# Gates and the retention half of the output projection by seven block products instead of eight

## The chip, the cores and the metric

The kernel runs on one core of one Trainium2 chip. The metric is the device time of one execution in microseconds (us). Of three runs of the kernel before the median is 1057.25 us (1056.99 to 1058.26).

## The reference, cut to what matters

One encoder layer on 1024 tokens of width 1024, all float32:

```python
h = rms_norm(x, norm_w) * (1 + scale) + shift          # adaLN(c) gives shift, scale, gate
r_q, r_k, r_v, r_g, m_cq, m_ckv, m_kr, m_g = split_cols(h @ w_in, SPLIT_SIZES)
# group A: 8 retention heads, both directions, group norm, then
ret_out = o * silu(r_g)                                # r_g: 1024 columns
# group B: latent attention with 8 heads
cq, ckv = rms_norm(m_cq, q_norm_w), rms_norm(m_ckv, kv_norm_w)     # 384 and 256 columns
q, kv = cq @ w_uq, ckv @ w_ukv                         # then per-head norms, rotary, softmax
mla_out = rms_norm(att, mla_out_norm_w) * silu(m_g)    # m_g: 1024 columns
x = x + gate * (concatenate([ret_out, mla_out]) @ w_out)
```

## The kernel before, in words

Every float32 product is made of three TensorE products of rounded halves: `split` (lines 75 to 82) makes a high part on ScalarE (line 80) and the rest, the low part, on GpSimd or VectorE (line 81); `mm3` (lines 64 to 67) then adds high x high, high x low and low x high into one accumulator. The accumulators are the eight banks of PSUM: four under the tag `acc`, four under `sm`. `h` lies in SBUF, feature by token, as eight pairs `hh`, `hl` of 128 x 1024. Weight pages come through `wpage` (line 84): load into `wr` (two buffers), split into `wh` and `wl` (seven buffers each), all in the pool `ring`.

The stages in order: the features `h` and the first retention projection (to about 82 us); four retention groups of two heads (line 330), each with a loop over eight token tiles (line 336: projection of 24 products, rotary, scores, states), a reverse scan over the states (line 397), the retention gate (from line 404: two pages, 96 products of 128 x 512, SiLU into `sg`), and the output part (line 416: two halves of four tiles; statistics, normalisation, transposes, line 444 multiplies by the gate, and the result goes to DRAM as `retD`). Then the latents (line 505: `cq` with 384 columns, `ckv` with 288, per token tile 24 products, norm, four transposes, high and low part into `cqh`, `cql`, `ckh`, `ckl`, which stay in SBUF). The eight latent gates (`mla_gate`, line 449) are written down in two parts, before and after the latents; they go to DRAM as `mgD`. `gate_column` (line 496) multiplies eight 512 KB pages on VectorE for the adaLN gate. Then the retention half of the output projection (line 557: `retD` is loaded and split, 8 x 2 x 24 products, residual added, stored as `xyD`), the pages of `w_uq` and `w_ukv` (line 577), the up-projections (line 595; lines 606 and 616 take the tag `wr` for the squares), attention, and the second half of the output projection.

The order written down is not the order issued: at the end a planner simulates the program, and each engine's stream is arranged by what is ready in that simulation, earlier lines first. Engines then work their streams strictly in order. SP issues the loads and most stores, ScalarE some stores. Pools are stacks from the left and the right end of SBUF; a pool that is opened where a closed one lay waits, tile by tile, for the tiles whose bytes it takes (`reuse_waits="tile"`).

## Time and profile before

| | |
|---|---|
| median of three runs | 1057.25 us |
| profiled execution | 1057.49 us |
| its span, first to last instruction | 1055.3 us |
| TensorE products (PE) | 1018.1 us busy, 5736 products |
| VectorE (DVE) | 581.4 us busy |
| ScalarE (ACT) | 426.0 us busy |
| GpSimd (POOL) | 404.1 us busy |
| mean granted clock of TensorE | 0.988 |

A product's row gives its latency; the next one starts before it ends, so rates are read from starts. PEld is the weight load, which overlaps the products. Behind a group's or an instruction's time stands the idle time of its engine before it, and what ended it.

### The profile page before, as it was taken

How to read it: one execution, taken by the hardware profiler on the slowest of the kernel's cores; microseconds unless marked ns; L12 is line 12 of the kernel's file. 1: busy time of each engine (PE TensorE's matmuls, PEld its weight loads, DVE VectorE, ACT ScalarE, POOL GpSimd, SP SyncE). 2: the span in 40 equal slices, each digit the busy share in tenths (PEclk: the TensorE clock that was granted, in tenths of full speed). 3: DMA queues.
4: the chain of work that ended last, by engine and by line, in shares of the span. 5: the costliest groups of instructions: out<-in, count | busy, mean ns of one | idle time of the engine just before them, and what ended most of it. 6: DMA issues, size and time to landing. Idle time of an engine off the chain costs nothing.

```text
span 1055.3 us, 15223 instructions
## 1 busy us (share of the span) xinstructions
PE 1018.1 (96%) x5736; PEld 888.3 (84%) x5736; DVE 581.4 (55%) x1390; ACT 426.0 (40%) x800; POOL 404.1 (38%) x311
## 2 busy tenths in 40 slices
PE   5899999999999999999999999989999999989998
PEld 4687887888888888998888889879889999878887
DVE  7996546444643534336302116777877777883342
ACT  6654213312321322124322006577767776772100
POOL 2233315213411411224633217943466555873210
PEclk8899999999999999999999999999999999998999
DMA  9721103101110212224654520100000000003522
GB/s 365 264 64 57 41 1 120 41 2 62 63 36 20 85 47 73 102 84 136 201 171 153 183 85 11 41 1 2 20 21 21 2 20 22 21 20 120 169 101 70
DMA packets 30744, 82.27 MB, mean 78 GB/s; under 512 B 3536, under 2 KB 4560, under 8 KB 30672
## 3 DMA queue, kind: packets, MB, share of 16 engines
q1 hardware_dynamic: 25920, 72.92, 20.4%
q10 hardware_dynamic: 4752, 8.39, 2.2%
q8 instruction: 45, 0.74, 0.3%
q14 instruction: 27, 0.22, 0.1%
HBM read 64.52 MB, written 16.78 MB: 77 GB/s over the span
## 4 chain that ended last, share of the span: by engine, by line
PE 82%; DVE 11%; DMA 2%; ACT 2%; issue 2%; POOL 2%; ACTq 0%; DVEq 0%; POOLq 0%
PE acc L65 13%; PE acc L66 13%; PE acc L67 13%; PE pt L739 4%; PE sp L65 4%; PE sp L66 4%; PE sp L67 4%; PE po L66 3%; PE po L67 3%; PE po L65 3%; DVE x L178 2%; DMA wa<-w_ada 2%; PE sm L425 2%; PE sm L424 1%; PE sm L65 1%
## 5 line engine op out<-in xcount | busy, mean ns | idle before, releaser
L81 POOL TENSOR_TENSOR wl<-wr,wh 128x1024 fp32r<-128x1024 f32 (+2 forms) x51 | 115.2, 2268 | 173.2 <-ACT wh L80 148.9
L65 PE MATMUL acc<-wh,hh 128*128 128x512 f32 (+2 forms) x352 | 130.8, 372 | 1.7 <-ACT hh L189 1.7
L66 PE MATMUL acc<-wl,hh 128*128 128x512 f32 (+2 forms) x352 | 130.3, 370 | 0.0
L67 PE MATMUL acc<-wh,hl 128*128 128x512 f32 (+2 forms) x352 | 126.4, 368 | 2.1 <-DVE hl L190 2.1
L725 POOL TENSOR_SCALAR pr<-pr,st 128x1024 f32<-128x1024 f32 x62 | 72.0, 1165 | 101.1 <-DVE st L724 75.5
L65 PE MATMUL acc<-hh,wh 128*128 128x512 f32 x256 | 101.0, 395 | 1.7 <-ACT v L345 1.7
L742 DVE TENSOR_TENSOR pl<-pt,ph 128x512 fp32r<-128x512 f32 x128 | 85.3, 683 | 31.2 <-ACT ph L741 31.1
L66 PE MATMUL acc<-hl,wh 128*128 128x512 f32 x256 | 100.9, 394 | 0.0
L67 PE MATMUL acc<-hh,wl 128*128 128x512 f32 x256 | 100.6, 393 | 0.0
L80 ACT CAST wh<-wr 128x1024 fp32r<-128x1024 f32 (+2 forms) x55 | 53.8, 982 | 104.1 <-PE sm L66 45.1
L741 ACT CAST ph<-pt 128x512 fp32r<-128x512 f32 x128 | 73.1, 591 | 26.6 <-PE pt L739 24.6
L720 DVE TENSOR_REDUCE st<-sp 128x1 f32<-128x1024 f32 x62 | 75.4, 1216 | 6.5 <-PE sp L67 6.4
L66 PE MATMUL po<-pl,vh 128*128 128x256 f32 x256 | 76.5, 299 | 2.1 <-DVE pl L742 2.0
L723 ACT ACTIVATE pr<-sp,st 128x1024 f32<-128x1024 f32 x62 | 69.5, 1121 | 20.8 <-DVE st L721 20.5
L65 PEld LDWEIGHTS acc<-wh,hh 128*128 128x128 f32 x352 | 67.2, 191 | 10.9 <-ACT hh L189 2.1
L67 PEld LDWEIGHTS acc<-wh,hl 128*128 128x128 f32 x352 | 66.0, 188 | 11.1 <-DVE hl L190 3.0
L66 PEld LDWEIGHTS acc<-wl,hh 128*128 128x128 f32 x352 | 67.3, 191 | 8.7
L739 PE MATMUL pt<-ident,pr 128*128 128x128 f32 x496 | 70.2, 274 | 4.0 <-DVE st L724 2.7
L65 PE MATMUL po<-ph,vh 128*128 128x256 f32 x256 | 73.3, 286 | 0.0
L67 PE MATMUL po<-ph,vl 128*128 128x256 f32 x256 | 72.8, 284 | 0.0
L360 POOL TENSOR_TENSOR rb<-t,t 128x128 f32<-128x128 f32 x32 | 14.8, 464 | 135.0 <-PE sm L370 73.4
L739 PEld LDWEIGHTS pt<-ident,pr 128*128 128x128 f32 x496 | 57.9, 141 | 8.5 <-issue 2.9
(353 smaller groups left out, 2474.2 us busy)
## 6 DMA issues: line engine op xcount, KB each, us to landing
...
retD<-ro SPq DMA_DIRECT2D x16, 256.0 KB, 2.1
...
```

The lines of the kernel that those rows point to most:

```text
L65: T.matmul(out, lh, rh, start=first, stop=False, **kw)
L66: T.matmul(out, lh, rl, start=False, stop=False, **kw)
L67: T.matmul(out, ll, rh, start=False, stop=last, **kw)
L80: A.copy(out=hi, in_=raw)
L81: eng.tensor_tensor(out=lo, in0=raw, in1=hi, op=ALU.subtract)
L178: V.scalar_tensor_tensor(out=wa, in0=wa, scalar=1.0, in1=sc, op0=ALU.mult, op1=ALU.mult, accum_out=mp[:, i:i + 1])
L720: V.tensor_reduce(out=st_[:, 0:1], in_=sp, op=ALU.max, axis=AX.X)
L723: A.activation(pr, sp, AF.Exp, bias=st_[:, 1:2], scale=sc_, accum_out=st_[:, 2:3])
L725: G.tensor_scalar(out=pr, in0=pr, scalar1=st_[:, 3:4], scalar2=0.0, op0=ALU.mult, op1=ALU.add)
L739: T.transpose(tp[:, ts_(q)], pr[:, ts_(half * 4 + q)], ident)
L741: A.copy(out=ph[half][:, :, c_], in_=tv)
L742: V.tensor_tensor(out=pl[half][:, :, c_], in0=tv, in1=ph[half][:, :, c_], op=ALU.subtract)
```

## The change

A product of a 2 x 2 block weight with 2 x 2 blocks of `h` (features 0 to 511 and 512 to 1023, tokens likewise) takes seven block products with sums before and after instead of eight plain ones. This is done for all retention gates, for the latent gates of heads 4 to 7, and for the retention half of the output projection: `block_pair` makes two 128-row output tiles over all tokens, ten times. The block sums on the side of `h`, `U`, are made once, in the latents stage (`combos`, `combo4`), and for the output projection once more from the gated retention (`rgD` in DRAM), written over the same tiles. The latent gates of heads 0 to 3 stay plain products, one page in each retention group. The retention gate is applied in `block_pair`'s stage, to `retD` from DRAM. `gate_column` moves into retention group 2. The latents run half 1 first, are stored to DRAM and loaded again after the output projection; the ring is closed before the latents and opened again after the output projection. The diff, cut to its core:

```diff
-    hh = [p_h.tile([P, S], F32R, name=f"hh{k}", tag=f"hh{k}") for k in range(KT)]
-    hl = [p_h.tile([P, S], F32R, name=f"hl{k}", tag=f"hl{k}") for k in range(KT)]
+
+    hf = [[[p_h.tile([P, 512], F32R, name=f"h{n}{k}{z}", tag=f"h{n}{k}{z}") for n in "hl"] for z in range(2)]
+          for k in range(KT)]
+
+    def h_tok(k, t):
+        return [x[:, ts_(t % 4)] for x in hf[k][t // 4]]
...
+    def gate_column():
+        sc2 = p_ret.tile([P, D], F32, name="sc2", tag="sc2")
+        bcast_row(sc2, sc_col)
+        for k in range(KT):
+            wa = wa_tile(16 + k, p_ret, "wa", 1)
+            V.scalar_tensor_tensor(out=wa, in0=wa, scalar=1.0, in1=sc2, op0=ALU.mult, op1=ALU.mult,
+                                   accum_out=modg[:, k:k + 1])
+        V.tensor_tensor(out=modg, in0=modg, in1=bada[:, 16:24], op=ALU.add)
...
-        wg = [wpage(I["w_rg"][g][j], 1024, 4) for j in range(2)]
-        sg = p_ret.tile([P, 2, S], F32, name="sg", tag="sg")
-        for h in range(2):
-            for half in range(2):
-                ps = acc()
-                for k in range(KT):
-                    wh, wl = wg[k // 4]
-                    rh = hh[k][:, half * 512:half * 512 + 512]
-                    rl = hl[k][:, half * 512:half * 512 + 512]
-                    mm3(ps, wh[:, k % 4, ts_(h)], wl[:, k % 4, ts_(h)], rh, rl, k == 0, k == KT - 1)
-                A.activation(sg[:, h, half * 512:half * 512 + 512], ps, AF.Silu)
+        wg = wpage(I["w_mg1"][g], 1024, KT)
+        for half in range(2):
+            ps = acc()
+            for k in range(KT):
+                mm3(ps, wg[0][:, k], wg[1][:, k], *hf[k][half], k == 0, k == KT - 1)
+            mo = p_ret.tile([P, 512], F32, name="mo", tag="qkT", bufs=2)
+            A.activation(mo, ps, AF.Silu)
+            A.dma_start(out=mgD[g, :, half * 512:half * 512 + 512], in_=mo)
+        if g == 2:
+            gate_column()
...
-                V.scalar_tensor_tensor(out=ro, in0=tp, scalar=gnw[:, 2 * g + h:2 * g + h + 1],
-                                       in1=sg[:, h, half * 512:half * 512 + 512], op0=ALU.mult, op1=ALU.mult)
+                A.activation(ro, tp, AF.Copy, scale=gnw[:, 2 * g + h:2 * g + h + 1])
...
-    for n in range(MG0):
-        mla_gate(n, p_ret, "qkT")
...
+    s_lw = ExitStack()
+    p_r2 = s_lw.enter_context(tc.tile_pool(name="ring2", bufs=1, side="right", reuse_waits="tile"))
+    bn = ("11", "1", "21", "2", "4", "3", "22")
+    p_T = s_h.enter_context(tc.tile_pool(name="pT", bufs=1, side="left", reuse_waits="tile"))
+    U = {"11": [hf[k][0] for k in range(4)], "12": [hf[k][1] for k in range(4)],
+         "21": [hf[k][0] for k in range(4, 8)], "22": [hf[k][1] for k in range(4, 8)]}
+    for n in "123":
+        U[n] = [[p_T.tile([P, 512], F32R, name=f"T{n}{m}{k}", tag=f"T{n}{m}{k}") for m in "hl"] for k in range(4)]
+    U["4"] = U["12"]
+    s_lat = ExitStack()
+    p_lw = s_lat.enter_context(tc.tile_pool(name="latw", bufs=1, side="left", reuse_waits="tile"))
+    cqD = dram.tile([6, P, S], F32R, name="cqD")
+    ckD = dram.tile([4, P, S], F32R, name="ckD")
...
+    def put(dst, x, eng):
+        hi, lo = dst
+        A.copy(out=hi, in_=x)
+        eng.tensor_tensor(out=lo, in0=x, in1=hi, op=ALU.subtract)
+    def tmp(i):
+        return p_lw.tile([P, 512], F32, name=f"x{i}", tag=f"x{i}")
+    def whole(i, blk, k):
+        x = tmp(i)
+        G.tensor_tensor(out=x, in0=U[blk][k][0].bitcast(F32), in1=U[blk][k][1].bitcast(F32), op=ALU.add)
+        return x
+    def combos(k):
+        a, b, d = whole(0, "11", k), whole(1, "12", k), whole(2, "22", k)
+        V.tensor_tensor(out=a, in0=b, in1=a, op=ALU.subtract)
+        put(U["1"][k], a, V)
+        V.tensor_tensor(out=b, in0=d, in1=b, op=ALU.subtract)
+        put(U["3"][k], b, V)
+        V.tensor_tensor(out=d, in0=d, in1=a, op=ALU.subtract)
+        put(U["2"][k], d, V)
+    def combo4(k):
+        a, b = whole(0, "2", k), whole(1, "21", k)
+        V.tensor_tensor(out=a, in0=a, in1=b, op=ALU.subtract)
+        put(U["4"][k], a, V)
+    lat = []
+    for nm, parts_, dd, wts in (("w_cq", ((0, 384),), cqD, qnw), ("w_ckv", ((0, 256), (256, 288)), ckD, kvnw)):
+        w = []
+        for j in range(4):
+            raw = p_r2.tile([P, 2 * n], F32, name="wr", tag="wr", bufs=2)
+            SY.dma_start(out=raw, in_=I[nm][j])
+            w.append(split(raw, (("p (k n) -> p k n",), {"k": 2}), f"{nm}h{j}", f"{nm}l{j}", p_r2))
+        lat.append((n, w, parts_, dd, wts))
+    for half in (1, 0):
...
+                if half == 1 and q % 2 == 1:
+                    combos(2 * unit + q // 2)
+                elif half == 0 and unit == 0:
+                    combo4(q)
...
+                hi = p_lw.tile([P, 512], F32R, name="sth", tag="sth", bufs=2)
+                lo = p_lw.tile([P, 512], F32R, name="stl", tag="stl", bufs=2)
+                A.activation(hi, tp, AF.Copy, scale=wts[:, j:j + 1])
+                V.scalar_tensor_tensor(out=lo, in0=tp, scalar=wts[:, j:j + 1], in1=hi, op0=ALU.mult, op1=ALU.subtract)
+                SY.dma_start(out=dd[j, :, sl].bitcast(F32), in_=hi.bitcast(F32))
+                SY.dma_start(out=dd[nj + j, :, sl].bitcast(F32), in_=lo.bitcast(F32))
+    SY.dma_start(out=tabD[2], in_=krp)
+    s_lat.close()
+    s_lw.close()
...
+    so = ExitStack()
+    p_g = so.enter_context(tc.tile_pool(name="blk", bufs=1, side="right", reuse_waits="tile"))
+    wn = ("11", "S1", "12", "S2", "22", "S3", "S4")
+    W = {}
+    for i, n in enumerate(wn):
+        W[n] = [p_g.tile([P, 4, P], F32R, name=f"W{n}{m}", tag=f"W{n}{m}") for m in "hl"]
+        if i == 1:
+            raws0 = {b: p_g.tile([P, 512], F32, name=f"r{b}", tag=f"r{b}", bufs=2) for b in ("11", "21", "22", "12")}
+    sub, add = ALU.subtract, ALU.add
+    def block_pair(src, consume, raws=None):
+        r = raws or {b: p_g.tile([P, 512], F32, name=f"r{b}", tag=f"r{b}", bufs=2) for b in ("11", "21", "22", "12")}
+        for b in r:
+            SY.dma_start(out=r[b], in_=src[("11", "12", "21", "22").index(b)])
+        def wput(n, x, eng):
+            hi, lo = (y.rearrange("p k n -> p (k n)") for y in W[n])
+            A.copy(out=hi, in_=x)
+            eng.tensor_tensor(out=lo, in0=x, in1=hi, op=sub)
+        s1 = p_g.tile([P, 512], F32, name="ws1", tag="ws1", bufs=1)
+        wput("11", r["11"], G)
+        V.tensor_tensor(out=s1, in0=r["21"], in1=r["22"], op=add)
+        wput("S1", s1, V)
+        V.tensor_tensor(out=r["21"], in0=r["11"], in1=r["21"], op=sub)
+        wput("12", r["12"], G)
+        V.tensor_tensor(out=r["11"], in0=s1, in1=r["11"], op=sub)
+        wput("S2", r["11"], V)
+        wput("22", r["22"], G)
+        wput("S3", r["21"], V)
+        V.tensor_tensor(out=r["12"], in0=r["12"], in1=r["11"], op=sub)
+        wput("S4", r["12"], V)
+        def prod(ps, a, b, first, last):
+            wh, wl = W[a]
+            for k in range(4):
+                mm3(ps, wh[:, k], wl[:, k], *U[b][k], first and k == 0, last and k == 3,
+                    skip_group_check=True)
+        def ot(tag):
+            return p_g.tile([P, 512], F32, name=tag, tag=tag, bufs=1)
+        A_, C_ = acc(), acc()
+        B_, D_ = sm(), sm()
+        prod(A_, "11", "11", True, True)
+        c1 = ot("c1")
+        A.copy(out=c1, in_=A_)
+        prod(C_, "S1", "1", True, True)
+        prod(A_, "12", "21", False, True)
+        consume(0, 0, A_)
+        prod(B_, "S2", "2", True, True)
+        u2, u4 = ot("u2"), ot("u4")
+        V.tensor_tensor(out=u2, in0=c1, in1=B_, op=add)
+        V.tensor_tensor(out=u4, in0=u2, in1=C_, op=add)
+        prod(D_, "22", "4", True, True)
+        prod(B_, "S3", "3", False, True)
+        V.tensor_tensor(out=c1, in0=c1, in1=B_, op=add)
+        c22, c21 = (p_g.tile([P, 512], F32, name="cc", tag="cc", bufs=2) for _ in range(2))
+        V.tensor_tensor(out=c22, in0=c1, in1=C_, op=add)
+        consume(1, 1, c22)
+        V.tensor_tensor(out=c21, in0=c1, in1=D_, op=sub)
+        consume(1, 0, c21)
+        E_ = acc()
+        prod(E_, "S4", "22", True, True)
+        V.tensor_tensor(out=u4, in0=u4, in1=E_, op=add)
+        consume(0, 1, u4)
+    rgD = dram.tile([H, P, S], F32, name="rgD")
...
+    def gate(n0, dst, src):
+        def go(f, z, c_):
+            sl = slice(512 * z, 512 * z + 512)
+            g_ = c_ if c_ is not None and (f or z) else None
+            if g_ is None:
+                g_ = p_g.tile([P, 512], F32, name="cc", tag="cc", bufs=2)
+            A.activation(g_, c_, AF.Silu)
+            if src is not None:
+                ro = io_tile()
+                SY.dma_start(out=ro, in_=src[n0 + f, :, sl])
+                V.tensor_tensor(out=g_, in0=g_, in1=ro, op=ALU.mult)
+            A.dma_start(out=dst[n0 + f, :, sl], in_=g_)
+        return go
+    for i, p_ in enumerate((0, 1, 2, 3)):
+        block_pair(I["w_gb"][p_], gate(2 * p_, rgD, retD), raws0 if i == 0 else None)
+    for p_ in (4, 5):
+        block_pair(I["w_gb"][p_], gate(2 * p_ - 4, mgD, None))
...
+    def ublk():
+        return p_g.tile([P, 512], F32, name="ub", tag="ub", bufs=10)
+    def uload(blk, k):
+        x = ublk()
+        SY.dma_start(out=x, in_=rgD[k + 4 * (blk[0] == "2"), :, slice(0, 512) if blk[1] == "1" else slice(512, 1024)])
+        return x
+    eng = lambda k: V if k % 2 else G
+    t1s = []
+    for k in range(4):
+        a = uload("11", k)
+        put(U["11"][k], a, eng(k))
+        b = uload("12", k)
+        V.tensor_tensor(out=a, in0=b, in1=a, op=sub)
+        t1s.append(a)
+    for k in range(4):
+        put(U["1"][k], t1s[k], eng(k))
+    t2s = []
+    for k in range(4):
+        c = uload("21", k)
+        put(U["21"][k], c, eng(k))
+    for k in range(4):
+        d = uload("22", k)
+        V.tensor_tensor(out=t1s[k], in0=d, in1=t1s[k], op=sub)
+        put(U["2"][k], t1s[k], eng(k))
+    for k in range(4):
+        c = uload("21", k)
+        V.tensor_tensor(out=c, in0=t1s[k], in1=c, op=sub)
+        put(U["4"][k], c, eng(k))
+    for k in range(4):
+        a = uload("11", k)
+        V.tensor_tensor(out=a, in0=t1s[k], in1=a, op=sub)
+        put(U["3"][k], a, eng(k))
+    for k in range(4):
+        put(U["22"][k], uload("22", k), eng(k))
...
+    def residual(f0):
+        def go(f, z, c_):
+            sl = slice(512 * z, 512 * z + 512)
+            xt = io_tile()
+            SY.dma_start(out=xt, in_=I["xT"][f0 + f][:, sl])
+            V.scalar_tensor_tensor(out=xt, in0=c_, scalar=modg[:, f0 + f:f0 + f + 1], in1=xt, op0=ALU.mult, op1=ALU.add)
+            A.dma_start(out=xyD[f0 + f][:, sl], in_=xt)
+        return go
+    for p_ in range(4):
+        block_pair(I["w_ob"][p_], residual(2 * p_))
+    so.close()
     s_h.close()
-    p_o2 = so.enter_context(tc.tile_pool(name="reto2", bufs=1, side="left", reuse_waits="tile"))
-    ohl += [[p_o2.tile([P, S], F32R, name=f"o{n}{k}", tag=f"o{n}{k}") for n in "hl"] for k in range(2, KT)]
-    oh, ol = zip(*ohl)
-    for k in range(KT):
-        raw = raws[k] if k < 2 else p_o.tile([P, S], F32, name="wro", tag="wro", bufs=2)
-        SY.dma_start(out=raw, in_=retD[k])
-        A.copy(out=oh[k], in_=raw)
-        eng = V if k % 2 == 0 else G
-        eng.tensor_tensor(out=ol[k], in0=raw, in1=oh[k], op=ALU.subtract)
-    for f in range(KT):
-        wh, wl = wpage(I["w_out"][f][0], 1024, KT)
-        for z in range(2):
-            sl = slice(z * 512, z * 512 + 512)
-            ps = acc() if z == 0 else sm()
-            for k in range(KT):
-                mm3(ps, wh[:, k], wl[:, k], oh[k][:, sl], ol[k][:, sl], k == 0, k == KT - 1)
-            xt = p_o2.tile([P, 512], F32, name="xt", tag="xt", bufs=4)
-            SY.dma_start(out=xt, in_=I["xT"][f][:, sl])
-            V.scalar_tensor_tensor(out=xt, in0=ps, scalar=modg[:, f:f + 1], in1=xt, op0=ALU.mult, op1=ALU.add)
-            A.dma_start(out=xyD[f][:, sl], in_=xt)
+    s_ck, s_cq = ExitStack(), ExitStack()
+    p_ck = s_ck.enter_context(tc.tile_pool(name="latk", bufs=1, side="right", reuse_waits="tile"))
+    s_ring = ExitStack()
+    p_ring = s_ring.enter_context(tc.tile_pool(name="ring", bufs=7, side="right", reuse_waits="tile"))
+    p_lat = s_cq.enter_context(tc.tile_pool(name="latq", bufs=1, side="right", reuse_waits="tile"))
+    cqh, cql, ckh, ckl = ([pool.tile([P, S], F32R, name=f"{nm}{j}", tag=f"{nm}{j}") for j in range(n)]
+                          for pool, nm, n in ((p_lat, "cqh", 3), (p_lat, "cql", 3), (p_ck, "ckh", 2), (p_ck, "ckl", 2)))
+    for dd, his, los in ((cqD, cqh, cql), (ckD, ckh, ckl)):
+        for j in range(len(his)):
+            SY.dma_start(out=his[j].bitcast(F32), in_=dd[j].bitcast(F32))
+            SY.dma_start(out=los[j].bitcast(F32), in_=dd[len(his) + j].bitcast(F32))
+    krp, mtab["Cq"], mtab["Sq"] = (p_lat.tile([P, NT, 2, 16], F32, name=n, tag=n) for n in ("krp", "Cq", "Sq"))
+    for i, t_ in enumerate((mtab["Cq"], mtab["Sq"], krp)):
+        SY.dma_start(out=t_, in_=tabD[i])
...
+    s_ring.close()
     s_ck.close()
-    s_ring.close()
```

## Rows read from the trace of the kernel before

**Rows 1.** The page's busy times: us (share of the span) xinstructions.

```profile
PE 1018.1 (96%) x5736; PEld 888.3 (84%) x5736; DVE 581.4 (55%) x1390; ACT 426.0 (40%) x800; POOL 404.1 (38%) x311
```

**Rows 2.** The chain of waits on the page, by engine.

```profile
PE 82%; DVE 11%; DMA 2%; ACT 2%; issue 2%; POOL 2%; ACTq 0%; DVEq 0%; POOLq 0%
```

**Rows 3.** Windows: length, busy us (x) of PE, PEld, DVE, ACT, POOL, clock, DMA, GB/s.

```profile
345.00:432.00 87.00, 87.00 (x465) 74.11 (x463) 36.66 (x129) 23.08 (x42) 23.59 (x23) 1.00 0.19 64
432.00:515.00 83.00, 80.88 (x506) 76.94 (x505) 39.23 (x94) 27.43 (x72) 35.46 (x42) 1.00 0.35 117
515.00:635.00 120.00, 120.00 (x534) 99.77 (x533) 17.52 (x20) 22.93 (x28) 34.71 (x16) 1.00 0.47 161
635.00:700.00 65.00, 63.35 (x360) 57.25 (x359) 44.77 (x112) 41.68 (x95) 46.02 (x27) 1.00 0.05 19
```

**Rows 4.** The same window of line 65 alone: products, weight loads.

```profile
345.00:432.00 87.00, 38.19 (x98) 18.24 (x97) 1.00 0.19 64
```

**Rows 5.** Groups of products of the gates and the output: count, busy us, mean ns.

```profile
L65 PE MATMUL acc<-hh,wh 128*128 128x512 f32 x256 | 101.0, 395 | 1.7 <-ACT v L345 1.7
...
L65 PE MATMUL acc<-oh,wh 128*128 128x512 f32 x64 | 24.9, 389 | 0.0
...
L65 PE MATMUL sm<-oh,wh 128*128 128x512 f32 x64 | 24.9, 389 | 0.0
```

**Rows 6.** Timeline of TensorE in the output stage: start, duration.

```profile
545.74 0.39 PE L65 MATMUL acc<-oh,wh 128*128 128x512 f32 x1
...
551.18 0.39 PE L65 MATMUL acc<-oh,wh 128*128 128x512 f32 x1
```

**Rows 7.** Line 565, low parts of 1024 columns: ns min/median/max.

```profile
L565 DVE TENSOR_TENSOR ol<-wro,oh x4: 1224/1225/2107, 519.1 to 562.2; 128x1024 fp32r<-128x1024 f32 x4
...
L565 POOL TENSOR_TENSOR ol<-wro,oh x4: 2387/2400/3371, 521.2 to 565.0; 128x1024 fp32r<-128x1024 f32 x4
```

**Rows 8.** Timeline of VectorE, output part of the last group: start, duration, idle before.

```profile
392.57 0.42 DVE L380 TENSOR_TENSOR sT<-sm,mask 128x256 f32<-128x256 f32 x1 [4.38 <-PE sm L378]
...
401.48 0.49 DVE L430 BATCH_NORM_STATS2 bs<-o 128x6 f32<-128x128 f32 x2 [4.74 <-ACT o L427]
...
413.83 1.41 DVE L444 SCALAR_TENSOR_TENSOR ro<-sm,small,sg 128x512 f32<-128x512 f32 x2 [2.80 <-PE sm L442]
...
419.78 0.49 DVE L430 BATCH_NORM_STATS2 bs<-o 128x6 f32<-128x128 f32 x2 [3.16 <-ACT o L427]
...
430.24 1.41 DVE L444 SCALAR_TENSOR_TENSOR ro<-sm,small,sg 128x512 f32<-128x512 f32 x2 [4.10 <-PE sm L442]
```

**Rows 9.** Timeline of one latent tile, from its squares to its scaled copy.

```profile
446.60 0.49 ACT L524 ACTIVATE jk<-acc 128x384 f32<-128x384 f32 x1 [3.60 <-PE acc L67]
...
448.09 0.62 DVE L531 TENSOR_SCALAR cn<-acc,rr 128x384 f32<-128x384 f32 x1 [0.72 <-POOL rr L528]
```

**Rows 10.** Line 542, high part of a latent on ScalarE: ns min/median/max.

```profile
L542 ACT ACTIVATE ckh<-sm,small x4: 678/680/689, 493.5 to 512.6; 128x512 fp32r<-128x512 f32 x4
```

**Rows 11.** DMA issues: count, KB each, median us from issue to landing.

```profile
retD<-ro SPq DMA_DIRECT2D x16, 256.0 KB, 2.1
...
wr<-w_ukv SPq DMA_DIRECT2D x4, 384.0 KB, 3.1
```

**Rows 12.** Timeline about 505 us: GpSimd and VectorE side by side.

```profile
502.71 4.74 POOL L81 TENSOR_TENSOR wl<-wr,wh 128x1024 fp32r<-128x1024 f32 x2
...
503.45 1.70 DVE L491 TENSOR_TENSOR rp<-cn,Ck 128x32 f32<-128x32 f32 x1
505.07 2.42 DVE L492 TENSOR_TENSOR rp<-cn,Sk 128x32 f32<-128x32 f32 x1
```

**Rows 13.** Line 492, the same multiplication in all token tiles: ns min/median/max.

```profile
L492 DVE TENSOR_TENSOR rp<-cn,Sk x8: 185/186/2423, 485.2 to 509.5; 128x32 f32<-128x32 f32 x8
```

**Rows 14.** Groups by form, splits of 768 columns: count, busy us, mean ns.

```profile
L81 POOL TENSOR_TENSOR wl<-wr,wh 128x768 fp32r<-128x768 f32 x11 | 20.2, 1839 | 77.9 <-ACT wh L80 77.9
...
L80 ACT CAST wh<-wr 128x768 fp32r<-128x768 f32 x11 | 9.2, 837 | 58.9 <-PE sm L66 38.2 <-DMA xt<-xT 10.0 <-DMA wr<-w_uq 6.7
```

88 lines of the change are left out of this document (26 added, 62 removed).

## The prediction, made before the result was known

> **What bounds the kernel now.** I read the busy times first: TensorE is busy 1018.1 of 1055.3 us, VectorE 55%, ScalarE and GpSimd 40% [rows 1]. The chain of waits agrees: 82% of the path to the end is TensorE work [rows 2]. A share over the whole span can hide stages with another limit, so I cut the span at the stages [rows 3]. In the last retention group (345 to 432 us) and in the output half of retention (515 to 635) TensorE never rests; in the latent stretch (432 to 515) it rests 2.1 us, in the up-projections (635 to 700) 1.65. So a product taken out of these stages is worth its full pitch, as long as something is ready to take its place. That condition decides here. In the stretch 345 to 432, for instance, line 65 starts 98 times [rows 4], with lines 66 and 67 some 290 products, nearly all of gates: over 60 us of them are laid between the steps of a slow per-token chain. The change takes most of this filling away.
>
> **What the change removes.** Gates and retention output are now 256 x 3 products of the gates and (64 + 64) x 3 of the output [rows 5]: 1152, each 128 x 512. Afterwards four 128-column gate pages stay plain (192), and ten block pairs take 7 x 4 x 3 = 84 where 96 stood: 192 + 840 = 1032. The pitch is read between two starts 24 products apart, 545.74 and 551.18 us [rows 6]: 0.2267 us (the 0.39 us of a row is latency, which overlaps). 120 x 0.2267 = **27.2 us less**. The new products have the same form, so no more than that; nothing only if TensorE were not the limit there, which rows 3 exclude for the kernel as it is. The two rests named above, 3.7 us, lie in stretches that are rebuilt: I take them out and count idle time there anew.
>
> **What is hidden.** In steady state a block pair lasts 84 x 0.2267 = 19.0 us. VectorE does for it 4 block combinations, 4 low parts, 6 output sums and 4 multiplications: 18 operations of 512 columns, at half of the 1.225 us that 1024 take [rows 7], some 11 us. GpSimd does 3 low parts of 1.2 us by the same rows, ScalarE some 12 casts, copies and SiLUs and 4 issues, some 8 us. All have lead, because each weight tile is free again right after its product, most of a pair before its next use. I take 1 us for the ten pairs (0 to 3); without the cover it would be some 11 us a pair. The gate column (8 multiplications on VectorE, 8 loads in SP's queue ahead of the last group's weight pages) goes from the latents into group 2; a group leaves VectorE idle for half its time (37 of 87 us busy in the last one [rows 3]), so I take nothing. Splitting h into half tiles, and `ro` on ScalarE instead of VectorE, cost nothing: the same work on engines that wait. A retention group loses 48 of its 96 gate products and shrinks to some 76 us, in which VectorE's work still fits: 2 us for the groups together (0 to 6).
>
> **The end of retention.** After the last token's masked scores (392.57) VectorE's rows show the rest of the group up to the gate multiplication at 430.24 [rows 8]: 38 us. In it VectorE waits 4.74, 2.80, 3.16 and 4.10 us for TensorE's results, which stand behind filling products; without these some 3 of the 14.8 would be left, so the bare chain is some 26 us, and TensorE's own narrow products in it are an estimated 8. Today gate pages fill the gap. Afterwards only four latent products are there (4 x 24 of 384 columns, by columns 16.3 us, one per accumulator); the fifth must wait, since the first normalised tile lies on buffers of the retention output. So idle is between 26 - 8 - 16 = 2 us and 18 (if the planner has used the filling up among the tokens before, as it does today). I take 8, nearer to the lower end, because some filling will be left.
>
> **Latents to gates.** The gate pages that fill the latents today are gone; nothing can follow the last latent before its tail is through. From the squares on the accumulator to the scaled tile take 2.1 us (446.60 to 448.71) [rows 9]; then transposes 1, hi on ScalarE 0.7 [rows 10] and lo on VectorE the same, store 2.1 [rows 11], reload of block weights between that and the 3.1 of a larger page, then sum, cast and low part 1.8. The first block product needs only the transposes done (its weight tile lies on the scaled latents) and a cast: it starts some 5 us after the last latent and ends at 8. The second needs `r21` and `r22`, whose bytes are those of the staging tiles `sth` and `stl` until these are stored: it starts at 11. Idle 4 + 3 = **7 us** (3, if transposes and stores run earlier, to 10).
>
> **Gates to output.** During the last gate pair and the first output pair U is rewritten from DRAM: 28 loads of 256 KB, 28 casts, 28 low parts, 16 subtractions. Each U block has 6 x 2.7 = 16 us between its last old and its first new use, the whole some 33 us. VectorE's 14 low parts and 16 subtractions at 0.61 are 18 us, with weights and sums of the pairs some 33: just full. GpSimd's 14 at 1.2 are 17. I take 4 us (0 to 16).
>
> Here and in the latents VectorE and GpSimd work on the same kind of operation at once, which the kernel before hardly does. What that can cost: at 502.71 GpSimd runs two splits, 4.74 us, and two 32-column multiplications of VectorE beside them take 1.70 and 2.42 us [rows 12], where 0.19 is usual [rows 13]. A two-input operation can wait for a whole GpSimd one. If all were serial, the rewriting with its pairs' weights would need 18 + 17 + 14 = 49 us in 33, the upper bound of 16 above. In the latents 32 subtractions (20 us), 20 additions on GpSimd (24) and some 17 of small operations make 61 us in some 50: upper bound 10, and I take 3, as most of it has lead. The Trainium skill has this as a rule (SBUF — State Buffer, "Who interferes with whom"): a VectorE instruction with two SBUF inputs and a GpSimd instruction that reads SBUF exclude each other for the whole instruction. The trace agrees, with the 2.42 us; by the rule taken strictly both terms go to their upper bounds, the third case below.
>
> **Output to up-projections.** The dearest. Today the seven pages of `w_uq` and `w_ukv` are split during the output stage, in a ring of their own. Afterwards the ring is opened over the block pool. Adding up the pools' sizes from the right end, the first `wl` lies on `ws1` and `c1`, the second on `cc`; `c1` is free when the last `c21` is formed, about when the last product ends (T). Only then can GpSimd make the first low part, 1.84 us [rows 14]. There are two raw buffers, so each later page waits for a load of 3.1 [rows 11], a cast of 0.84 and a low part of 1.84 [rows 14], 5.8 us a turn: pages 0, 2, 4, 6 end at T + 2, 8, 14, 19.5, pages 1, 3, 5 at 4, 10, 15.5. Page 2 completes the first group of products at T + 8. Worse, the squares of the first tokens take the same two buffers (tag `wr`), so the first comes after page 5 (T + 16) and the second after page 6 (T + 20); until then four accumulators stay full. In these 20 us TensorE has some 8 us of work: **12 idle** (6, if pages come off earlier, to 16). The reload of the latents, 10 x 512 KB in SP's queue ahead of the pages, is hidden by the last output pair, as most of its buffers come free before.
>
> **Sum.** 1057.5 (the profiled execution's own time: span 1055.3 and 2.2 around it; the median of the runs, 1057.25, is the same within 0.03%) - 27.2 - 3.7 + 1 + 2 + 8 + 7 + 4 + 3 + 12 = 1063.6: **1064 us**, 0.6% slower. The products saved are real, but the borders that they used to fill take more.
>
> **The rivals.**
> - *The borders stay covered.* No border in rows 3 rests over 2.1 us today, and the planner reorders every engine's stream to keep it so. The place that decides is the page ring: if the low parts come off before T, so that the squares don't stand behind seven pages, this border costs 6; with it the others at their lower ends, 2 + 3, and 4 for the rest: 1057.5 - 30.9 + 15 = **1042**. For it: what the planner does today. Against: the filling is gone from three of the borders, and buffers that overlap can't be ordered away.
> - *The blocks' arithmetic becomes the bound.* VectorE and GpSimd strictly one after the other: 16 and 10 instead of 4 and 3, 19 more: **1083**. For it rows 12; against: most of this work has many microseconds of lead.
> - *No gain*: the products are saved, but a wait per product takes their place (an output sum late in VectorE's queue holds the accumulator), and a pair lasts 22 us as before: 1064 + 27 = **1091**. Against: another product stands between most sums and the next use of their accumulator.
>
> **Chances.** Forecast 0.50, covered borders 0.30, arithmetic 0.16, no gain 0.04. The forecast's own range is 1057 to 1072. Differences under 0.2% (2.1 us) can't be told from none here. Faster 0.30: nearly all of the covered case and the lowest edge of the forecast. Same 0.12: the rest of that case and the forecast's lower tail. Slower 0.58. The range reaches from the covered case to the arithmetic one, 1042 to 1083.
>
> **What would show it.** 120 fewer 512-column products at the same 0.2267 us. TensorE rests some 8 us in the last retention group, 7 between last latent and first block products behind the `sth` and `stl` stores and the loads of `r21` and `r22`, and 12 after the last output product, with GpSimd's `wl` as releaser of the page loads. If TensorE is busy through the start of the up-projections, my largest term is wrong and the kernel faster; if U's low parts release TensorE late in the first output pair, the third case holds; if pairs last well over 19.5 us, the fourth.

## The result, and the profile after

The changed kernel takes 1121.3 us (median of four runs, 1119.2 to 1121.6) against 1057.8 for the kernel before, run beside it: ratio 1.059, 95% interval 1.057 to 1.0615. It is slower, as forecast, but by 63 us instead of 6, and lies 38 us above the range. The profiled execution has a span of 1117.4 us, 62.1 more than before.

The busy times of after, which answer to [rows 1]:

```profile
PE 1012.2 (91%) x5616; PEld 876.4 (78%) x5616; DVE 725.6 (65%) x1588; ACT 477.3 (43%) x912; POOL 441.4 (40%) x351
```

120 matrix instructions fewer, exactly; busy time falls by only 6 us, because a product that starts alone or at a lower clock is busy longer (the last section has 0.52 us against 0.33 for the same shape). The chain of waits of after holds 69% TensorE work where [rows 2] had 82%, and VectorE now has 16% of it:

```profile
PE 69%; DVE 16%; POOL 4%; DMA 4%; issue 3%; ACT 2%; SPq 0%; ACTq 0%; POOLq 0%; DVEq 0%
```

The windows of after, by stage (columns as in [rows 3]: stretch, length, busy time of each engine, granted clock, DMA share, GB/s):

```profile
382.00:400.00 18.00, 9.46 (x56) 9.46 (x57) 12.55 (x22) 6.61 (x20) 12.21 (x11) 0.62 0.12 43
440.00:455.00 15.00, 5.12 (x19) 3.23 (x18) 5.26 (x18) 4.40 (x10) 5.17 (x10) 0.62 0.64 209
453.00:567.00 114.00, 113.85 (x493) 93.70 (x493) 84.34 (x110) 49.12 (x85) 35.46 (x25) 0.98 0.60 190
567.00:660.00 93.00, 82.39 (x347) 65.33 (x345) 68.89 (x91) 26.48 (x46) 28.94 (x20) 0.96 0.46 148
660.00:712.00 52.00, 23.47 (x93) 19.90 (x94) 11.16 (x31) 17.89 (x37) 21.15 (x10) 0.67 0.49 170
```

The six gate pairs (453 to 567) are full: 113.85 of 114 us, 19.0 a pair. Nearly all the loss is at the borders. Where, TensorE's own rows tell; each is the first instruction after a rest, whose length and releaser stand in brackets:

```profile
339.93 0.71 PE L392 MATMUL sm<-qkT 128*128 128x128 f32 x4 [0.73 <-ACT qkT L386]
378.37 2.20 PE L455 MATMUL sm<-ident,o 128*128 128x128 f32 x8 [3.72 <-DVE o L450]
390.54 0.90 PE L573 MATMUL sm<-ident,cn 128*128 128x128 f32 x3 [9.97 <-DVE cn L559]
451.93 0.79 PE L65 MATMUL acc<-hh,W11h 128*128 128x512 f32 x1 [7.27 <-ACT W11h L604]
585.86 0.79 PE L66 MATMUL sm<-hl,W22h 128*128 128x512 f32 x1 [5.01 <-DVE hl L503]
602.05 0.50 PE L66 MATMUL sm<-T3l,WS3h 128*128 128x512 f32 x1 [2.22 <-DVE T3l L503]
683.07 1.01 PE L65 MATMUL acc<-wh,cqh 128*128 128x384 f32 x2 [24.50 <-ACT wh L80]
```

A rest is not the whole price, so I also added up, from TensorE's rows of both kernels, how far each instruction starts behind the one before it beyond the usual pitch of its shape (512 columns 0.227 us, 384 0.173, 288 0.133, 256 0.120, 128 0.110). This *lost time*, after minus before, beside the prediction's terms (stretches of before: 82 to 345, 432, 515, 635 and the end; latents and their meeting of VectorE and GpSimd with the border to the gates, less the 2.1 us of idle; the up-projections less their 1.65). How the smallest gaps are counted moves a row by up to 5 us, the same way in every kernel; the differences between kernels hold to about 1 us:

| stage of after (us) | before | after | more | predicted |
|---|---|---|---|---|
| retention groups, 82 to 340 | 7.5 | 15.0 | 7.5 | 2 |
| end of retention, 340 to 400 | 1.2 | 21.7 | 20.5 | 8 |
| latents and border to gates, 400 to 455 | 3.5 | 14.4 | 10.9 | 7.9 |
| gate pairs, 455 to 567 | -0.1 | 1.1 | 1.2 | 1 |
| output pairs, 567 to 658 | (in the row above) | 12.8 | 12.8 | 4 |
| output to up-projections, and to the end | 16.0 | 52.5 | 36.5 | 10.4 |
| sum | 28.1 | 117.5 | 89.4 | 33.3 |

89.4 less the 27.2 saved is the 62 us of the spans. Four borders are worth following.

SP's queue at the last border (issues; a row of several gives the first start and the stretch they are issued in), and below it what SP waited for from 640 to 672 us (total, times, longest):

```profile
634.29 18.91 SPq L720 DMA_DIRECT2D io<-xT  x5
658.38 0.33 SPq L741 DMA_DIRECT2D cqh<-cqD  x1
668.50 0.32 SPq L741 DMA_DIRECT2D ckh<-ckD  x1
673.99 11.27 SPq L86 DMA_DIRECT2D wr<-w_uq  x3
```

```profile
SPq L720 <- DMA xyD<-io: 17.0, 4, 7.4
SPq L741 <- PE sm L67: 5.4, 1, 5.4
SPq L741 <- DMA xyD<-io: 7.2, 1, 7.2
```

The last product starts at 658.18. Three things hold SP in turn. Until 653.2 it stands at loads of x (line 720), each of which needs one of three buffers back from a store. Then it stands 5.4 us at the first latent load itself, until TensorE's last products: in the program's layout the first `cqh` tile lies over the last tile of T3, which they read. Six loads are issued from 658.38 on; the seventh, the first `ckh`, waits 7.2 us for a store of an `io` tile. Its bytes are not those of `io`; in the program it waits for nothing but the completion semaphore that it takes over from that store. The first page is issued at 673.99, and the first product that needs it starts at 683.07. Meanwhile, from 664 to 667 for instance, the DMA engines are the only thing working, at a share of 1.02 (the column before the last):

```profile
664.00:667.00 3.00, 0.00 (x0) 0.00 (x0) 0.00 (x0) 0.00 (x0) 0.00 (x0) 0.50 1.02 364
```

At the border from the latents to the gates SP issues the first raw blocks behind the last latents' stores:

```profile
444.91 0.32 SPq L581 DMA_DIRECT2D tabD<-krp  x1
446.90 0.41 SPq L580 DMA_DIRECT2D ckD<-stl  x1
447.36 3.02 SPq L600 DMA_DIRECT2D r<-w_gb  x4
```

At the end of retention GpSimd waits until the last tiles of retention have gone out, then makes three block sums ahead of the first roots that the latents wait for. (The row names `tabD<-Cq`, the store of a table issued right behind the last `retD` store; in the program the sums wait for the `retD` stores, over whose tiles `ro` the `x` tiles lie.)

```profile
384.31 3.70 POOL L510 TENSOR_TENSOR x<-hh,hl 128x512 f32<-128x512 f32 x3 [6.47 <-DMA tabD<-Cq]
387.96 1.80 POOL L556 TENSOR_TENSOR rr<-ss,neghalf 128x1 f32<-128x1 f32 x2
```

And in the rewriting of U the same VectorE operation takes 1.78 or 0.68 us, by which of the two engines started first. At 556.64 GpSimd did, and VectorE ends 0.55 us after it; at 560.06 VectorE did, and GpSimd takes 1.61 us instead of the 1.27 of its shortest:

```profile
557.15 1.78 DVE L503 TENSOR_TENSOR hl<-ub,hh 128x512 fp32r<-128x512 f32 x1
560.06 0.68 DVE L503 TENSOR_TENSOR T1l<-ub,T1h 128x512 fp32r<-128x512 f32 x1
```

```profile
556.64 1.74 POOL L503 TENSOR_TENSOR T1l<-ub,T1h 128x512 fp32r<-128x512 f32 x1
560.27 1.61 POOL L503 TENSOR_TENSOR T1l<-ub,T1h 128x512 fp32r<-128x512 f32 x1 [1.89 <-ACT T1h L502]
```

### The profile page after: what moved, and what is told of

It is laid out like the page before. It is cut to its first block, busy times and chain, and to the rows that moved or that the text cites. A ratio compares the mean times of both kernels' runs of the same rounds, so it can differ in the third digit from the quotient of the medians.

```text
span 1117.4 us, 15663 instructions
## 1 busy us (share of the span) xinstructions
PE 1012.2 (91%) x5616; PEld 876.4 (78%) x5616; DVE 725.6 (65%) x1588; ACT 477.3 (43%) x912; POOL 441.4 (40%) x351
## 4 chain that ended last, share of the span: by engine, by line
PE 69%; DVE 16%; POOL 4%; DMA 4%; issue 3%; ACT 2%; SPq 0%; ACTq 0%; POOLq 0%; DVEq 0%
PE acc L65 9%; PE acc L67 9%; PE acc L66 9%; PE pt L907 5%; PE sp L65 4%; PE sp L67 4%; PE sp L66 4%; PE po L66 3%; PE po L67 3%; PE po L65 3%; PE sm L66 2%; PE sm L67 2%; PE sm L65 2%; DVE x L182 2%; PE sm L438 2%
## 5 line engine op out<-in xcount | busy, mean ns | idle before, releaser
L65 PE MATMUL acc<-wh,hh 128*128 128x512 f32 x224 | 90.8, 405 | 2.6 <-ACT hh L194 1.7
L81 POOL TENSOR_TENSOR wl<-wr,wh 128x1024 fp32r<-128x1024 f32 (+1 forms) x23 | 53.1, 2319 | 101.2 <-ACT wh L80 90.7
L66 PE MATMUL acc<-wl,hh 128*128 128x512 f32 x224 | 90.2, 403 | 0.0
L67 PE MATMUL acc<-wh,hl 128*128 128x512 f32 x224 | 85.8, 396 | 2.0 <-DVE hl L195 1.8
L65 PE MATMUL sp<-kh,qh 96*128 96x512 f32 x124 | 54.2, 437 | 2.5 <-ACT pr L891 1.4
L65 PEld LDWEIGHTS acc<-wh,hh 128*128 128x128 f32 x224 | 43.2, 193 | 12.2 <-ACT hh L194 2.1
L66 PEld LDWEIGHTS po<-pl,vh 128*128 128x128 f32 x256 | 48.9, 191 | 3.7 <-DVE pl L910 2.6
L67 PEld LDWEIGHTS acc<-wh,hl 128*128 128x128 f32 x224 | 41.9, 188 | 11.2 <-DVE hl L195 2.8
L66 PEld LDWEIGHTS acc<-wl,hh 128*128 128x128 f32 x224 | 43.1, 193 | 8.6
L65 PEld LDWEIGHTS po<-ph,vh 128*128 128x128 f32 x256 | 49.0, 191 | 1.0
```

What stands on the lines that cost most here:

```text
L65: T.matmul(out, lh, rh, start=first, stop=False, **kw)
L66: T.matmul(out, lh, rl, start=False, stop=False, **kw)
L67: T.matmul(out, ll, rh, start=False, stop=last, **kw)
L81: eng.tensor_tensor(out=lo, in0=raw, in1=hi, op=ALU.subtract)
```

## The experiments

All start from the changed kernel (1121.3). Times are medians of four runs, ratios are to the kernel before, with 95% intervals. "Lost time" is the sum defined above.

### The last border

**a1: pages ahead of the latents.**

```diff
-    (reload of cqD, ckD; tables)
     wuq = [wpage(I["w_uq"][j], 768, 1) for j in range(3)]
...
+    (reload of cqD, ckD; tables)
```

> The changed kernel takes 1121.3 us; after its last output product TensorE rests 24.5 us. Here only the order changes: the seven pages of w_uq and w_ukv are asked for ahead of the ten latent tiles. Theory Q (the in-order load queue, 5.2 MB of latents ahead of the pages): the first page is cast some 3 us after the last product instead of 24, but the first group still needs 3 MB of w_cq latents, 8 to 9 us at the 364 to 398 GB/s of that stretch, so the first product starts at about +12: 1110 us (1105 to 1115). Rival R (the page ring of two raw buffers over the output tiles sets the pace, whenever the pages are asked for): within 3 us of 1121.

1113.4 us, 1.051 [1.0497, 1.0528]: theory Q, at the upper end of its range. The order counts, but less than expected; SP still waits 4.4 us at the first latent load for the last product and 8.0 at a later one for a store. The first product starts 4.7 us after the last one, then TensorE rests 10.5 for the third page, which again stands behind nine latent loads (671.72). One blockage is traded for another in the same queue.

**a2: reload early in SP's queue.**

```diff
-            xt = io_tile()
+            xt = ublk() if f0 == 6 else io_tile()
...
+    reload(ckD, ckh, ckl, (0, 1)); two pages; reload(cqD, cqh, cql, (2, 1, 0))
```

> The last output pair's x tiles come out of the ten ub buffers, so that no x load waits for a store in front of the latents; then two ckv tiles, two pages, the cq tiles last to first, the other pages. Theory Q: most of the reload and two pages lie under the last output pair, the first product starts 3 to 8 us after the last one instead of 24.5: 1100 us (1095 to 1106), below the kernel with the pages alone first. Rival V (the volume: the buffers come free only with the last pair, so 5.2 MB still pass after it, 14 us at 380 GB/s): 1112 us (1108 to 1117). Rival R (page ring): within 3 us of 1121.

1113.5 us, 1.051 [1.0497, 1.0528]: the time of rival V, but not for its reason. The first latent load is issued at 638.21, the second 26.6 us later, and the view of SP's waits says for what:

```profile
664.77 0.33 SPq L743 DMA_DIRECT2D ckl<-ckD  x1
```

```profile
SPq L743 <- DMA xyD<-ub: 26.2, 1, 26.2
```

This edit put the last pair's x tiles into `ub`, and in the program's layout the first `ckl` tile lies over one of them. So the load waited for its own bytes, which the edit itself had made late, and everything behind it in the queue waited with it. The reload was still not early, so this run doesn't decide between queue and volume.

**b1: reload by GpSimd's queue.**

```diff
-            SY.dma_start(out=his[j].bitcast(F32), in_=dd[j].bitcast(F32))
+            G.dma_start(out=his[j].bitcast(F32), in_=dd[j].bitcast(F32))
...
+    (ckD first; the three tables at the low end of latq, so that no latent tile lies over T3)
```

> The ten latent tiles are asked for by GpSimd's queue (which has nothing else to issue and is idle in the last output pair), ckv first; the three tables that lie over the last T3 tile move to the low end of their pool, so that no latent tile waits for the last product; pages stay in SP's queue. The kernel with the same reload earlier in SP's queue took 1113.5 us: its second ckv load stood until 664.8 us behind the store of the last output tile. Theory Q2 (what holds the reload is the queue and the completion lanes that SP and ScalarE's stores share, not its buffers or its volume): 4.8 of 5.2 MB pass under the last pair, the first product starts 2 to 6 us after the last one: 1098 us (1093 to 1104). Rival V (buffers come free only at the end of the last pair, 14 us of transfers after it whoever asks): 1111 us (1108 to 1116).

1102.0 us, 1.042 [1.039, 1.0445]: theory Q2, 19.3 us less for the same bytes. GpSimd issues all ten by 649.2, under the last pair, and the first product follows after 8.3 us:

```profile
668.41 1.01 PE L65 MATMUL acc<-wh,cqh 128*128 128x384 f32 x2 [8.33 <-ACT wh L80]
```

So with this layout the buffers do come free before the end. But the edit changes three things at once: the queue, the order (ckv first), and the place of the tables, by which no latent tile lies over T3 any more. The queue takes away the x loads and the semaphores shared with stores, the place takes away the 5.4 us at the first tile. No run moves the queue alone or the tables alone; the 19.3 us are the price of the three together.

**c2: page buffers and squares of their own** (on top of b1).

```diff
+        raw = p_uw.tile([P, 768], F32, name="wr", tag="wr", bufs=4)
-        sq = p_ring.tile([P, 4, 96], F32, name="sq2", tag="wr", bufs=2)
+        sq = p_uw.tile([P, 4, 96], F32, name="sq2", tag="sq", bufs=2)
```

> On top of the reload in GpSimd's queue (1102.0 us; 8.3 us rest after the last output product, then 16.7 us of small rests in the up-projections): the raw pages of w_uq and w_ukv get four buffers of their own on the left, over T2, and the squares two others, so that squares no longer wait behind seven pages for the same two buffers. Theory P (the page turn: raw buffers, cast, low part, and squares behind pages, as the prediction put it): four pages are there when the last product ends, the two numbers fall to some 5 and 9: 1092 us (1088 to 1097). Rival L (low parts: the first must wait for the last output sum's buffer and GpSimd takes 1.8 us for each of seven): 2 to 4 us less only, 1099 us.

1101.4 us, 1.0405 [1.039, 1.042], not told apart from b1; theory P is out, and rival L's 1099 is missed as well. In the stage itself lost time falls from 17.0 to 11.4 (the squares behind the pages were worth 5.6 us); the rest of 7.9 stays (SP issues the first page at 661.54, behind the x loads and after the last product), and attention, which the edit doesn't touch but whose order the planner writes anew, loses 3.5.

**d2: the first pages by GpSimd's queue too** (on top of c2).

```diff
-        SY.dma_start(out=raw, in_=src)
+        q.dma_start(out=raw, in_=src)    # q: GpSimd for the first four, ahead of the w_cq latents
```

> On top of pages and squares in buffers of their own (1101.4 us, 7.9 us rest after the last output product; its first page was asked for at 661.5 us, 0.3 us after that product, because the last x tile's load stood before it in SP's queue): the first four pages are asked for by GpSimd's queue ahead of the latents. Theory Q3 (the pages too are held by SP's order, not by buffers or volume): the rest falls to 1 to 3 us: 1095 us (1092 to 1098). Rival V2 (volume: pages and latents together don't fit under the last pair): within 2 us of 1101.

1100.2 us, 1.039 [1.0365, 1.041]: the time of rival V2. The rows of GpSimd's queue, two windows and ScalarE's rows show that volume is only part of it:

```profile
648.81 0.76 POOL L747 DMA_DIRECT2D wr<-w_uq  x1 [10.70 <-PE sm L67]
654.50 0.55 POOL L752 DMA_DIRECT2D ckh<-ckD  x1
```

```profile
652.00:656.00 4.00, 4.00 (x19) 3.34 (x18) 2.03 (x3) 0.00 (x0) 3.11 (x6) 1.00 0.63 124
664.00:668.00 4.00, 0.00 (x0) 0.00 (x0) 2.81 (x5) 0.68 (x1) 0.54 (x1) 0.62 1.04 401
```

```profile
644.72 22.49 ACTq L722 DMA_DIRECT2D xyD<-io  x5
667.32 3.03 ACT L80 CAST wh<-wr 128x768 fp32r<-128x768 f32 x4 [22.29 <-DMA cqh<-cqD]
```

The pages lie over T2, which the last pair still reads, so GpSimd stands at them until 648.81 and again until 652.89, and the latents behind them are issued 16 us later than in c2 (654.50 instead of 638.55). The DMA engines, over 0.9 busy from 640 to 660 in c2, are at 0.56 and 0.63 from 648 to 656 here, and full from 660 on, after the last product. The first page was asked for early, but its cast stands on ScalarE behind the last stores. So a block in a queue is part of V2's time here too. 5.2 MB of latents and 1.6 MB of pages take 17 us at the 400 GB/s of these windows, an estimate; whether that fits under the last pair when nothing stands ahead of it, no run shows. The cause of the last 8 us stays open.

### End of retention, latents, border to the gates

**a4: the latents' block-sum additions on VectorE.**

```diff
-        G.tensor_tensor(out=x, in0=U[blk][k][0].bitcast(F32), in1=U[blk][k][1].bitcast(F32), op=ALU.add)
+        V.tensor_tensor(out=x, in0=U[blk][k][0].bitcast(F32), in1=U[blk][k][1].bitcast(F32), op=ALU.add)
```

> The 20 additions that put high and low part of a block together during the latents on VectorE instead of GpSimd. Theory X (each addition of 1.3 us on GpSimd holds up VectorE by 1.1 us and stands ahead of the reciprocal roots in GpSimd's queue, 5 of the 10 us rest at 381 us): VectorE works 12 us more but is held up 20 us less, roots come at once: 1112 us (1107 to 1117). Rival C (VectorE is the bound of the latents by count): no change or slower, 1120 to 1127 us.

1124.6 us, 1.062 [1.0605, 1.064], slower by 3, the time of rival C. But the stage did gain, some 5 of the 9 us expected: lost time from the end of retention to some 12 us after the first gate product is 31.8 instead of 37.3. Attention lost 6.6, most of it in one rest that the changed kernel doesn't have:

```profile
977.56 0.80 PE L65 MATMUL sp<-kh,qh 96*128 96x512 f32 x1 [6.00 <-ACT pr L891]
```

On every engine the planner's order in attention differs between the two programs. So the whole time does not speak for rival C, and the stage speaks for theory X.

**b2: the latents' working tiles off the retention's bytes.**

```diff
-                a_ = p_lw.tile([P, 384], F32, name="cn", tag="cn", bufs=5)
+                a_ = p_r2.tile([P, 384], F32, name="cn", tag="cn", bufs=5)
...                (so too jk, ss, rr and x0 to x2)
```

> The latents' working tiles (squares, roots, scaled tiles cn, x of the block sums) move to the pool of the latents' weights, over the retention's old weight ring instead of over its output buffers. Theory B (TensorE's 10 us rest at 381 us and part of the 3.7 before it come from these bytes: squares, roots and the first scaled tile can't begin before the last retention tile is stored): the four latent products at the end of retention are followed by more, 17 us of idle there fall to 5 to 8: 1110 us (1105 to 1114). Rival O (GpSimd's queue: block-sum additions stand ahead of the roots wherever the tiles lie): 2 to 4 us less only, 1118 us.

1113.2 us, 1.051 [1.048, 1.0545]. Lost time at the end of retention falls from 21.7 to 7.9, theory B; the latents fill the gap, as the window shows. They run out earlier, and from 400 us to 15 us after the first gate product 19.4 are lost instead of 15.6:

```profile
382.00:400.00 18.00, 18.00 (x128) 17.88 (x127) 10.01 (x30) 6.85 (x21) 7.57 (x9) 1.00 0.21 74
```

**b4: the staging tiles there too** (on top of b2).

```diff
-                hi = p_lw.tile([P, 512], F32R, name="sth", tag="sth", bufs=2)
+                hi = p_r2.tile([P, 512], F32R, name="sth", tag="sth", bufs=2)
```

> As the kernel with the latents' working tiles in the right pool, and their staging tiles sth and stl there too, under the ub tiles that are needed last. Theory B: the first block pair's weight tiles and raw blocks then lie over nothing that the last latents write; the rest of 7.3 us before the first block product falls to some 2 to 3 (transposes, and TensorE's last squares): 1105 us (1100 to 1109), 5 below the kernel without it. Rival: the rest is the latents' own tail (squares, root on GpSimd, scaled tile, transposes), then within 2 us of that kernel.

1138.7 us, 1.075 [1.073, 1.0775]: 25 slower than b2, by neither theory. The larger pool pushes the raw tiles of `w_cq` down onto bytes of the retention pool, and their loads now stand behind the last retention stores:

```profile
367.08 11.93 SPq L458 DMA_DIRECT2D retD<-ro  x4
379.11 0.91 SPq L535 DMA_DIRECT2D wr<-w_cq  x2
```

```profile
384.60 1.65 PE L65 MATMUL acc<-w_cqh,hh 128*128 128x384 f32 x4 [7.01 <-ACT w_cqh L80]
```

Without latent products as filling, the end of retention and the first latents (340 to 420) lose 41.9 us. Whether the bytes or the planner's order hold the loads isn't told apart, but it prices the filling that the prediction spoke of.

**c3: first raw blocks by GpSimd's queue** (on top of b2).

```diff
-            SY.dma_start(out=r[b], in_=src[("11", "12", "21", "22").index(b)])
+            (G if raws else SY).dma_start(out=r[b], in_=src[("11", "12", "21", "22").index(b)])
```

> On top of the latents' working tiles in the right pool (1113.2 us; TensorE then rests 8.2 us before the first block product): the four raw blocks of the first gate pair are asked for by GpSimd's queue instead of SP's, where they stood behind the stores of the last latents. Theory S (they wait in the queue, not for their buffers or for TensorE): asked for 3 to 4 us earlier, 1109 us (1106 to 1111). Rival Z (the first weight tile lies on the staging tiles and has to wait for their stores all the same): within 1.5 us of 1113.

1117.7 us, 1.055 [1.053, 1.057]: 4.5 slower, by neither theory. GpSimd issues them behind its last block sums, 3.7 us later than SP had in b2 (436.62), so theory S got no test; the rest grows from 8.2 to 13.4:

```profile
439.07 1.26 POOL L510 TENSOR_TENSOR x<-T2h,T2l 128x512 f32<-128x512 f32 x1 [0.63 <-DMA tabD<-krp]
440.28 2.38 POOL L600 DMA_DIRECT2D r<-w_gb  x4
```

**d1: the last stores by ScalarE's queue** (on top of b2).

```diff
+                Q = SY if half or unit == 0 else A
-                SY.dma_start(out=dd[j, :, sl].bitcast(F32), in_=hi.bitcast(F32))
+                Q.dma_start(out=dd[j, :, sl].bitcast(F32), in_=hi.bitcast(F32))
...                (staging tiles lowest, ub with 9 buffers)
```

> On top of the latents' working tiles in the right pool (1113.2 us, 8.2 us rest before the first block product): the last latents' stores go out by ScalarE's queue, so that SP reaches the first pair's raw blocks before them, and the staging tiles lie below the first weight tile instead of under it (one ub buffer less pays for that). Theory S (the raw blocks wait behind stores in SP's in-order queue): the raw blocks are there when the last latent ends, the rest falls to 3 to 5 us: 1109 us (1106 to 1111). Rival G (GpSimd and ScalarE still have the last block sums to make before the first weight cast; putting the raw loads behind those cost 4.5 us): within 1.5 us of 1113.

1111.8 us, 1.0505 [1.048, 1.0525]: rival G. SP now issues the first raw blocks from 430.6 on, and TensorE still rests 8.2 us; ScalarE casts the last block sum (U4) first, and the weight after it:

```profile
442.94 0.62 ACT L503 CAST hh<-x 128x512 fp32r<-128x512 f32 x1 [2.90 <-DVE x L527]
443.47 0.61 ACT L606 CAST W11h<-r 128x512 fp32r<-128x512 f32 x1
```

**e3: U4's sums inside the first block pair** (on top of all edits together, d4 below).

```diff
-                    combo4(q)
...
+        for k in range(4 if raws else 0):
+            a, b = (p_g.tile([P, 512], F32, name="ub", tag="ub", bufs=9) for _ in range(2))
...
+            put(U["4"][k], a, V)
```

> On top of all edits together (1081.8 us, 13.9 us rest before the first block product). There the raw blocks are asked for from 426 us on, but the cast of the first weight block stands on ScalarE behind the four casts of the rewritten U4, one each 2.8 us of VectorE's block sums, until 443.6. Here these four sums move into the first block pair, behind its first weight casts, in tiles of ub. Theory G (the block sums in the in-order queues hold the first cast): the first product starts some 4 us after the last latent, the second waits some 4 more for VectorE (WS1 behind the sums): 1076 us (1072 to 1079). Rival T (the latents' own tail or the raw loads hold it): within 1.5 us of 1082.

1086.9 us, 1.0265 [1.024, 1.029], 5 slower than d4 and outside both forecasts. At the place in question theory G holds: the rest before the first block product falls from 13.9 to 3.6, lost time from 400 to the full pairs from 21.3 to 16.5. But `ub` is now asked for earlier and so lies elsewhere in its pool, and the ckv tiles come to lie over the last pair's sums and x tiles: GpSimd issues its first ckv load at 641.0, after the last product, and that border goes from 8.0 to 17.5:

```profile
433.67 0.80 PE L65 MATMUL acc<-hh,W11h 128*128 128x512 f32 x1 [3.58 <-ACT W11h L598]
641.02 0.54 POOL L753 DMA_DIRECT2D ckh<-ckD  x1 [9.94 <-DVE io L722]
654.80 0.98 PE L65 MATMUL acc<-wh,cqh 128*128 128x384 f32 x2 [17.51 <-DMA cqh<-cqD]
```

### The rewriting of U, the products, and all together

**a3: U's low parts all on VectorE.**

```diff
-    eng = lambda k: V if k % 2 else G
+    eng = lambda k: V
```

> All 28 low parts of the rewritten U on VectorE, none on GpSimd. Theory X (VectorE and GpSimd exclude each other: VectorE operations of 0.68 us took 1.78 beside GpSimd's, 1.1 us lost for each of 14 low parts, 15 us, against 14 x 0.61 = 8.5 us of added work): TensorE's rests of 5.0 and 2.2 us at the start of the output shrink, 1115 us (1111 to 1118). Rival C (VectorE is simply full by count there, so 8.5 us of more work end the stage later): 1127 us (1123 to 1130).

1114.7 us, 1.053 [1.051, 1.0545]: 6.6 less, theory X. More work on the fuller engine makes it faster. The rests of 5.0 and 2.2 us are gone; the longest left at this border is 1.75. By itself the run can't tell the exclusion from GpSimd's own slower pace (1.27 us alone, where VectorE takes 0.68); the rows of 1.78 and 0.68 above show the exclusion.

**b3: the last product of each pair twice** (that output block holds it twice).

```diff
-        prod(E_, "S4", "22", True, True)
+        prod(E_, "S4", "22", True, False)
+        prod(E_, "S4", "22", False, True)
```

> The last of each pair's seven products (S4 by 22) is run twice into the same bank, so 12 more products of 512 columns a pair and 120 in all, the number that the change took out; that output block holds the product twice. Theory T (each block pair is limited by TensorE, so the products taken out were worth their pitch): 120 x 0.2267 = 27.2 us more, 1148 us (1145 to 1151). Rival W (in the output pairs the rewriting of U or VectorE is the limit, so products there are hidden): less, 12 to 20 us, 1133 to 1141 us.

1149.4 us, 1.085 [1.083, 1.088]: 28.1 more, theory T. A product is worth its pitch in these pairs, so the saving of 27 us is real where nothing else rests.

**c4 and d4: together.** c4 joins b1, c2, a3, b2 and c3; d4 joins b1, c2, d2, a3, b2, d1 and a4.

> All that helped together: reload in GpSimd's queue, pages and squares in buffers of their own, U's low parts on VectorE, the latents' working tiles in the right pool, the first raw blocks in GpSimd's queue; the arithmetic is that of the changed kernel. If the losses are separate and add up: 1121.3 - 19.3 - 9 - 6.6 - 8.1 - 4 = 1074 us (1068 to 1081), still above the 1058 of the kernel before. If they lean on each other (a wait removed uncovers the next): 1085 to 1095.

> All together: reload and first pages in GpSimd's queue, pages and squares in buffers of their own, U's low parts and the latents' block-sum additions on VectorE, the latents' working tiles in the right pool, their last stores by ScalarE's queue. The earlier sum of edits, with the first raw blocks behind GpSimd's block sums, took 1084.8 us. If each does what it should: 9 less before the first block product (13.1 to 4), 6 less after the last output product, 4 less in the latents: 1066 us (1060 to 1072). If the last block sums hold the first weight cast whoever loads: 1074 to 1080.

c4 1084.8 us, 1.025 [1.023, 1.026], at the edge of its second case: the losses lean on each other. d4 1081.8, 1.021 [1.020, 1.023]: outside both of its forecasts, nearest to the second. Together the edits take back 39.5 of the 63.5 us lost; the kernel before stays ahead. In d4 lost time is still 18 above before from 400 to the first full pairs, 15 from the last output product on, 8 in the retention groups, 6 at the end of retention and 4.5 in the pairs: together 51 against 27 saved. U4's casts hold the first weight until 443.56 (e3 moved them):

```profile
443.56 0.61 ACT L606 CAST W11h<-r 128x512 fp32r<-128x512 f32 x1
```

## Why the prediction was wrong, and where it was right

- **Products saved, 27.2 us: right.** 120 fewer; b3 gives 28.1 for putting as many back.
- **Pairs at 19.0 us, 1 us for all: right.** The gate pairs are full; the "no gain" rival is out.
- **Output to up-projections, 12 us: this step failed**, with 36.5. The sentence was that the reload "is hidden by the last output pair, as most of its buffers come free before". It was not hidden: its first load was issued at 658.38, after the start of the last product. Most buffers do come free before, as b1's layout shows, but SP works in order, and I left out what it stands at: the x loads that wait for stores, then the reload's own first tile, over T3, which comes free last (5.4 us), then a store's semaphore (7.2 us). One late tile at the head of a queue makes the whole reload late. b1, which removes all three at once, prices them at 19.3 us; b1, c2 and d2 leave a rest of 8 us whose cause is open. The term that I did work out, pages and squares turning in two buffers, was no more than 5.6 us in its stage (c2), against 12.
- **End of retention, 8 (2 to 18): mis-sized**, 20.5. The chain and the missing filling were right, also that the first scaled tile lies on retention's bytes; b2 shows this placement alone to be worth 13.8. I missed that the same bytes hold the block sums, that these stand ahead of the roots on GpSimd, and that TensorE then starts at half clock.
- **Latents to gates, 7, and the meeting in the latents, 3: near in size (10.9 with the lower clock, against 7.9), wrong in detail.** Rest 7.27, but not "behind the `sth` and `stl` stores" for their bytes, which cost the later raw blocks only 1.0 us: in the changed kernel the raw loads are issued behind the stores in SP's queue, and once they aren't (d1) the casts of U4 hold the first weight (e3).
- **Gates to output, 4 (0 to 16): the rival was nearer.** "VectorE and GpSimd strictly one after the other" is what the rows show, 1.78 against 0.68 us, with 12.8 of its 16 us; a3 takes 6.6 back. The rule that I cited (the Trainium skill, SBUF — State Buffer, "Who interferes with whom") agrees with the trace: VectorE loses 1.1 us to a GpSimd operation that takes 1.27 alone, when GpSimd started first. I let "most of it has lead" outweigh rows and rule, and there was no lead.
- **Retention groups, 2 (0 to 6): low**, 7.5. No experiment was made on it; TensorE rests nine times, 6.0 us in all, behind ScalarE's copy `qkT` (339.93 above is one of 0.73), against 0.7 in the kernel before. That gate products used to cover these rests is argued, not shown.
- **The sum.** The losses came together: the terms' upper ends (3 + 6 + 18 + 10 + 16 + 10 + 16 us, less 30.9) would have given 1106; the rest is the reload, which had no range at all. That the change came out slower was forecast, but the term that made it dearest in the forecast is not the one that did.
